# A mixture-of-experts block: the fixed first pass in tiles of 64 and 32 from raw weights, with six loads lent the room of the split parts

## The chip, the cores and the metric

The kernel runs on one core of a Trainium2 chip. It is one launch, and its time is the device time in microseconds (us). The core's engines are TensorE (PE; its weight loads are shown apart as PEld), VectorE (DVE), ScalarE (ACT), GpSimd (POOL) and SyncE (SP), with 16 DMA engines beside them. Each engine runs its own instructions in the order in which the kernel lists them, and waits for other engines by semaphores.

## The reference

The reference is a stack of three blocks over 512 tokens of width 1024: one with convolutions and a linear recurrence, one with attention, and a mixture of experts. The change touches the last alone. In outline:

```
logits = h1 @ w_router + b_router            # 512 tokens, 32 experts
top 4 experts of each token, softmax over the 4 -> gate
for each expert e, on its tokens:
    g, l = split(x @ w_gate_up[e] + b_gate_up[e])     # 1024 -> 2048
    a = swiglu(g, l)                                  # 1024
    out[token] += gate * (a @ w_down[e] + b_down[e])  # 1024 -> 1024
```

All is float32. The weights of one expert are 12 MB, so the 32 experts are 384 MB of the 503 MB that the kernel moves.

## The kernel before

The experts are run in 32 passes. Pass 0 is expert 0 always (`STATIC = 1`); the other experts are put into passes by their number of tokens, so that a pass has a fixed kind. A pass gathers the rows of its tokens from DRAM (an indirect DMA on POOL, `rows_of`, L1571), transposes them on PE, multiplies and scatters the result back. There are four kinds:

- *large* passes hold one tile of 128 places. Their weights are split into a high part (`whi`, cast on ACT, L142) and a remainder (`wlo`, subtracted on DVE, L143), and a unit of 1 MB takes three products of four matmuls each, 128x512 (L1930 for gate_up, L1941 for down). Pass 0 is of this kind.
- *SMALL* passes hold 64 places, from the raw float32 weights (L1912). In the trace a unit has 8 records of a 64-column tile with 512 columns moving.
- *TINY* passes hold 32 places, raw too: 16 records of a 32-column tile with 256 columns moving.
- *PAIRS* (passes 3 and 9) hold 128 places from split weights and 32 more from the raw ones, so each of their units is worked once in either way.

The program goes by blocks. Block b has the 8 gate_up units of pass b and then the 4 down units of pass b-1. Beside them, `beside(b)` lists small work that is put before or in the middle of a given unit: finding the rows of the next pass (`place`, `fetch`), gathering them (`gather`), transposing them (`xpose`, `xparts`), the SwiGLU (`glu`), the transposed activations (`at_T`, `at_parts`) and the scatter (`finish`).

Weights come in loads of 1 MB, all on SP's queue, in the order of use. `Weights` holds a list of loads to do and a list of free buffers (`slots`, 12 in the mixture of experts: 2, 7 from L1351 and 3 from L2062). `issue()` (L117) takes the oldest free slot and puts the next load into it. For a unit that is split, the slot is free again once the two casts have read it, and `split()` issues the next load there; for a raw unit `release(slot)` does that after PE's last product. The high and low parts have buffers of their own, three pairs (`wpart0` to `wpart2`), which serve the layers ahead too. The first 12 loads are gate_up of pass 0 (8) and down of pass 0 (4); then come gate_up of pass 1, gate_up of pass 2, down of pass 1, and so on. From pass 1 on, a load's address depends on `pm_i`, the list of which expert is in which pass; SP reads that into a register with `value_load` and waits for it there.

The stage ahead of pass 0 ends with the normalised rows `hr` being stored to `h_d` (from which the gathers read) and `acc_d` (to which the results are added), also on SP's queue (L1423, L1425). The router's result gives places (`posb`), from which a one-hot (`oh`), PE products with it (`pidx`) and a few DVE operations give the row numbers `ix` of a pass's tokens. Twelve matmuls on a constant (`warm`, L198) stand on PE between that and pass 0.

Of the kernel before, what the change touches and what calls it, by code (L numbers as in the profile page):

```python
# [9 lines left out]
F32 = mybir.dt.float32  # L10
# [4 lines left out]
OP = mybir.AluOpType  # L15
# [19 lines left out]
STATIC = 1  # L35
PAIRS = (3, 9)
SMALL = (1, 2, 4, 6, 8, 10, 12, 14, 16, 18, 20, 22, 24, 26, 27, 28, 29, 30, 31)
TINY = (1, 4, 10)
# [3 lines left out]
def _tables():  # L42
# [35 lines left out]
    for r, q_ in enumerate([*PAIRS, *large, *[q_ for q_ in SMALL if q_ not in TINY], *TINY, *range(STATIC)]):  # L78
        moe[:, q_] = r
        moe[:, 32 + q_] = 160 if q_ in PAIRS else 32 if q_ in TINY else 64 if q_ in SMALL else 128  # L80
    moe[:, 64] = p // 64
# [10 lines left out]
class Weights:  # L92
# [3 lines left out]
    def __init__(self, nc, pools, slots):  # L96
        self.nc, self.slots = nc, list(slots)
        self.parts = [(pools, f"wpart{i}") for i in range(2)]
        self.todo, self.raw, self.part = [], [], []
        self.last, self.used = 0, 0  # L100

# [48 lines left out]
    def release(self, slot):  # L150
        self.slots.append(slot)
        self.issue()

# [17 lines left out]
def block_kernel(ctx, tc, A, out, dbg=None, upto=99):  # L171
# [60 lines left out]
    def kn(k, n):  # L232
        return lambda t: t[:, :k * n].rearrange("p (k n) -> p k n", k=k)
# [58 lines left out]
    for p in range(NE):  # L292
        k = 1 + (p in PAIRS)
        PASSES.append(list(range(ni, ni + k)))
        ni += k
# [10 lines left out]
    def paired(p):  # L306

        return p not in PAIRS and p not in TINY

# [3 lines left out]
    def add_unit(p, dn, u, of, late=0):  # L313
        def src():
            w = of(p)[dn]
            return rows2(w[256 * u:256 * u + 256, :], paired(p)) if dn else w[128 * u:128 * u + 128, :]
        W.add((kn(2, 1024) if dn else flat, src), split="both" if p in PAIRS else p not in SMALL,
              late=late)
# [1145 lines left out]
    for hf in range(2):  # L1464
# [3 lines left out]
        for i in range(4):  # L1468
# [17 lines left out]
            if hf:  # L1486
                stats1(i)
                if i:
                    top4(i - 1)
                else:  # L1490
                    W.ahead(1)
            elif i == 1:
                biases()
            elif i == 2:
                W.ahead(1)
                next(terms)
            elif i == 3:
                next(terms)
    logits_T(3)
    norm1(3)  # L1500
# [82 lines left out]

    oh_ = onehot(posb[:, :, 0:1])
    first = rows_of(rows_at(oh_, lambda i: aux[:, :, i, 0], 0, 2))

# [180 lines left out]
    def small(n):  # L1767

        if PASS_OF[n] in TINY or PLACES[n][1]:
            return 4  # L1770
        return 2 if PASS_OF[n] in SMALL else 0

# [37 lines left out]
    def xpose(n):  # L1810
        it = its[n]
        if small(n):
            it["pt"] = transposed_rows(it["xg"])
        else:
            pt = pss("pxt") if n == 0 else None
            it["pt"] = [transposed(it["xg"], a, pt[:, a, :] if n == 0 else psa("pxt")) for a in range(2)]

# [74 lines left out]
    def small_products(n, dn, u, w, half):  # L1892
# [15 lines left out]
        for k in range(2):  # L1908
# [4 lines left out]
            if k == 0:  # L1913
                half()
        W.release(slot)

# [30 lines left out]
    def beside(b):  # L1947
# [23 lines left out]
        if b == 0:  # L1971
            before[4].append((place, 1))
            midst[4].append((fetch, 1))
            before[5] += [(gather, 1), (late_gates, 0)]
            before[8].append((place, 2))
            midst[7].append((xpose, 1))
            before[8].append((xparts, 1))
        else:
# [29 lines left out]
    def further_tiles():  # L2008
# [4 lines left out]
        with tc.For_i(0, total, 1) as it:  # L2013
            with tc.manual_schedule():
# [48 lines left out]
    W.prefetch()  # L2063
    its[0] = {"oh": oh_, "cols": lambda i: aux[:, :, i, 0], "ix": first[0], "xg": first[1],
              "se": selr[:, 0:1].to_broadcast([128, 128]), "acc": {}, "ac": {}, "pa": {}, "parts": {}}
    for p, dn, u in units(1):
# [7 lines left out]
    warm(12, bias_p)  # L2074
    xpose(0)
    xparts(0)
    for b in range(NE + 1):
# [120 lines left out]
```

## Time and profile before

| | |
|---|---|
| time, median of 3 runs | 1894.53 us (1890.97 to 1894.7) |
| profiled execution, its own time | 1889.37 us |
| its span in the profile | 1887.6 us |
| mean granted clock of PE | 0.951 of full speed |
| PE busy | 1682.0 us, 89% |
| DVE busy | 1127.2 us, 60% |
| ACT busy | 752.8 us, 40% |
| DMA | 503.49 MB, 267 GB/s over the span |

The mixture of experts takes the time from about 800 us on. A busy engine is not a bound by itself: the share is an average over stages with different limits. Which one ends last in a stage is read from what each engine waits for there, and from how full the DMA engines are in it (a share of 1.00 means that all 16 have packets at all times).

### The profile page before, as it was taken

The numbers are of one execution on the slowest core, as the hardware profiler recorded it, in microseconds if no ns is written. First come the engines' busy times: TensorE is split into PE (matmuls) and PEld (weight loads), VectorE is DVE, ScalarE is ACT, GpSimd is POOL, SyncE is SP. The second block draws the span as 40 slices with busy tenths as digits, with TensorE's granted clock in tenths as the row PEclk, the third lists the DMA queues.
The fourth block names the chain that finished last, engine by engine and source line by source line (L and its number), as shares of the span: only waits on it lengthen the run. The fifth ranks groups of instructions, "written<-read, shape, count | busy, mean of one in ns | idle before, by whom it ended". The sixth has DMA issues, their size and how long they took to land. (4 is left out here: it accounts for less than half of the span.)

```text
span 1887.6 us, 22807 instructions
## 1 busy us (share of the span) xinstructions
PE 1682.0 (89%) x8479; PEld 1120.8 (59%) x8479; DVE 1127.2 (60%) x1467; ACT 752.8 (40%) x894; POOL 512.6 (27%) x400
## 2 busy tenths in 40 slices
PE   4899785979998899978999999999999999999885
PEld 3687573758787677854565565666456556642221
DVE  6799983775746555756565466566547545641113
ACT  5233542742335545333354354445335534520001
POOL 3899994550311221311111101110011011110102
PEclk8999897989999899989899999999999999999998
DMA  8322221336131003769999999999999999999993
GB/s 300 90 73 73 78 90 45 111 133 210 59 109 56 1 1 111 296 266 364 379 394 410 399 413 397 394 403 414 418 404 407 406 404 393 405 407 397 407 414 136
DMA packets 127442, 503.49 MB, mean 267 GB/s; under 512 B 15227, under 2 KB 57785, under 8 KB 79713
## 3 DMA queue, kind: packets, MB, share of 16 engines
q1 hardware_dynamic: 115568, 475.24, 63.7%
q0 software_dynamic: 11024, 25.39, 4.9%
q8 instruction: 68, 1.11, 0.2%
q10 hardware_dynamic: 736, 1.38, 0.2%
q14 instruction: 46, 0.37, 0.1%
HBM read 488.56 MB, written 19.84 MB: 269 GB/s over the span
## 5 line engine op out<-in xcount | busy, mean ns | idle before, releaser
L143 DVE TENSOR_TENSOR wlo<-wraw,whi 128x2048 fp32r<-128x2048 f32 (+1 forms) x201 | 456.9, 2282 | 177.8 <-ACT whi L142 172.1
L142 ACT CAST whi<-wraw 128x2048 fp32r<-128x2048 f32 (+1 forms) x201 | 379.5, 1890 | 222.2 <-DMA wraw<-w_down 93.9
L1912 PE MATMUL pg<-wraw,xTs 128*64 128x512 f32 (+1 forms) x1664 | 277.1, 518 | 15.0 <-DMA wraw<-w_gate_up 14.8
L1912 PEld LDWEIGHTS pg<-wraw,xTs 128*64 128x64 f32 (+1 forms) x1664 | 85.5, 126 | 166.2 <-issue 109.8
L1912 PE MATMUL pg<-wraw,ats 128*64 128x512 f32 (+1 forms) x832 | 146.2, 527 | 8.9 <-DMA wraw<-w_down 6.7
L1660 DVE TENSOR_SCALAR lp<-pg 128x512 f32<-128x512 f32 (+1 forms) x47 | 31.1, 661 | 191.9 <-ACT sg L1659 190.3
L563 POOL TENSOR_TENSOR acc<-acc,sparel 128x512 f32<-128x512 f32 x91 | 133.3, 1465 | 7.7 <-ACT acc L552 0.2
L1667 POOL DMA_INDIRECT acc_d<-y,back x20 | 33.1, 1656 | 374.9 <-ACT y L1886 357.1
L1571 POOL DMA_INDIRECT xg<-h_d,ix x34 | 53.9, 1584 | 235.3 <-PE pg L1912 109.8
L1930 PE MATMUL pg<-whi,xTh 128*128 128x512 f32 x416 | 117.1, 403 | 0.4 <-issue 0.4
L1930 PE MATMUL pg<-whi,xTl 128*128 128x512 f32 x416 | 115.8, 400 | 0.0
L1930 PE MATMUL pg<-wlo,xTh 128*128 128x512 f32 x416 | 113.3, 394 | 0.0
L1667 POOL DMA_INDIRECT acc_d<-y,ix x13 | 26.1, 2011 | 309.0 <-ACT y L1889 210.2
L556 DVE SCALAR_TENSOR_TENSOR pc<-v,C,pc 128x512 f32<-128x512 f32 x144 | 101.6, 747 | 2.1 <-ACT pc L552 0.8
L1659 ACT ACTIVATE sg<-pg 128x512 f32<-128x512 f32 (+1 forms) x47 | 25.7, 573 | 183.4 <-PE pg L1912 99.9
L561 POOL TENSOR_SCALAR sparel<-v,C 128x512 f32<-128x512 f32 x91 | 93.8, 1031 | 14.5 <-DVE V L478 5.8
L1930 PEld LDWEIGHTS pg<-whi,xTh 128*128 128x128 f32 x416 | 76.3, 189 | 26.5 <-issue 10.3
L1930 PEld LDWEIGHTS pg<-wlo,xTh 128*128 128x128 f32 x416 | 78.9, 190 | 17.9
L1930 PEld LDWEIGHTS pg<-whi,xTl 128*128 128x128 f32 x416 | 77.3, 190 | 16.6
L1941 PE MATMUL pg<-whi,ath 128*128 128x512 f32 x208 | 73.9, 438 | 12.8 <-ACT whi L142 12.8
L1912 PEld LDWEIGHTS pg<-wraw,ats 128*64 128x64 f32 (+1 forms) x832 | 41.2, 127 | 73.7 <-issue 47.6
L1941 PE MATMUL pg<-wlo,ath 128*128 128x512 f32 x208 | 71.7, 428 | 11.8 <-DVE wlo L143 11.8
(661 smaller groups left out, 3289.3 us busy)
## 6 DMA issues: line engine op xcount, KB each, us to landing
wraw<-w_gate_up SPq DMA_DIRECT2D x256, 1024.0 KB, 20.5
wraw<-w_down SPq DMA_DIRECT2D x128, 1024.0 KB, 21.7
wraw<-w_in SPq DMA_DIRECT2D x17, 1024.0 KB, 5.3
wraw<-w_out SPq DMA_DIRECT2D x8, 1024.0 KB, 6.1
mraw<-mod_w SPq DMA_DIRECT2D x7, 1024.0 KB, 12.5
wraw<-w_in SPq DMA_DIRECT2D x14, 512.0 KB, 5.1
wraw<-pw_w SPq DMA_DIRECT2D x4, 1024.0 KB, 5.2
wraw<-mod_w SPq DMA_DIRECT2D x4, 1024.0 KB, 5.1
```

What stands on the lines that cost most here:

```text
L142: self.nc.scalar.copy(out=hi[:, c], in_=t[:, c])
L143: self.nc.vector.tensor_tensor(out=lo[:, c], in0=t[:, c], in1=hi[:, c].bitcast(F32), op=OP.subtract)
L556: dve.scalar_tensor_tensor(out=acc[:, c, :] if j == 29 and not np_ else st_["o"], in0=v[:, j:j + S], scalar=dw_col(j, c), in1=st_["o"], op ...
L561: pool.tensor_scalar(out=pr_, in0=v[:, j:j + S], scalar1=dw_col(j, c), scalar2=0.0, op0=OP.mult, op1=OP.add)
L563: pool.tensor_tensor(out=acc[:, c, :], in0=acc[:, c, :], in1=pr_, op=OP.add)
L1571: pool.indirect_dma_start(out=xg, out_offset=None, in_=h1_d[:, :], in_offset=bass.IndirectOffsetOnAxis(ap=ix[0:w], axis=0), bounds_check=S ...
L1659: act.activation(out=sg, in_=v2[:, :, :, 0], func=AF.Sigmoid, scale=1.702)
L1660: dve.tensor_scalar(out=lp, in0=v2[:, :, :, 1], scalar1=-6.0, scalar2=8.0, op0=OP.max, op1=OP.min)
L1667: pool.indirect_dma_start(out=dst, out_offset=bass.IndirectOffsetOnAxis(ap=ix, axis=0), in_=y, in_offset=None, bounds_check=nt * S - 1, oo ...
L1912: pe.matmul(o, l, t[:, c0:c0 + n_], start=False, stop=u == 3 and k == 1 if dn else u == 7)
L1930: pe.matmul(it["acc"][c // 2][:, c % 2, :], l, r[:, 512 * c:512 * c + 512], start=False, stop=u == 7 and j == 2)
L1941: pe.matmul(it["acc"][2][:, c, :], l, r[:, c0:c0 + 512], start=False, stop=end)
```

## The change

- The places of expert 0 are 96 and not 128, as a tile of 64 and a tile of 32. Both use the raw weights. `PASSES[0]` has two members, and all that indexed pass 1 by number goes by `PASSES[1][0]`.
- A raw unit of a pass with two tiles is released after the last of them. The down weights of pass 0 are loaded in two pieces of 4 KB for each partition (`128x2x1024`) in place of one of 8 KB.
- Pass 0 has no casts on ACT and no subtractions on DVE: 12 of either go.
- Two one-hots, two sets of row numbers and two gathers stand ahead of pass 0, where one of each stood. The offsets of the second tile's places are a DVE operation more (`pl1`).
- `W.lend()`, called after the last product of the attention block's output layer, puts the six halves of the part buffers on the list of free slots, once: they are not given back by `release`. Three of them take the three down loads of pass 0 that had no room, the other three the first gate_up loads of pass 1. There are 18 slots for the loads up to then, and 12 after.

```
--- before.py
+++ after.py
@@ -77,7 +77,7 @@
     large = [q_ for q_ in range(STATIC, NE) if q_ not in PAIRS and q_ not in SMALL]
     for r, q_ in enumerate([*PAIRS, *large, *[q_ for q_ in SMALL if q_ not in TINY], *TINY, *range(STATIC)]):
         moe[:, q_] = r
-        moe[:, 32 + q_] = 160 if q_ in PAIRS else 32 if q_ in TINY else 64 if q_ in SMALL else 128
+        moe[:, 32 + q_] = 160 if q_ in PAIRS else 32 if q_ in TINY else 64 if q_ in SMALL else 96 if q_ < STATIC else 128
     moe[:, 64] = p // 64
     moe[:, 65] = p // 32
 
@@ -97,7 +97,7 @@
         self.nc, self.slots = nc, list(slots)
         self.parts = [(pools, f"wpart{i}") for i in range(2)]
         self.todo, self.raw, self.part = [], [], []
-        self.last, self.used = 0, 0
+        self.last, self.used, self.lent = 0, 0, []
 
     def add(self, *loads, split=True, n=2048, pieces=1, late=0):
 
@@ -148,8 +148,15 @@
         self.rest = [lambda i=i: piece(i) for i in range(1, pieces)]
 
     def release(self, slot):
-        self.slots.append(slot)
-        self.issue()
+        if slot not in self.lent:
+            self.slots.append(slot)
+            self.issue()
+
+    def lend(self):
+
+        self.lent = [(pool, tag + x) for pool, tag in self.parts for x in "hl"]
+        self.slots += self.lent
+        self.prefetch()
 
     def ahead(self, n):
         while len(self.part) < n and self.ready():
@@ -290,7 +297,7 @@
 
     PASSES, ni = [], 0
     for p in range(NE):
-        k = 1 + (p in PAIRS)
+        k = 1 + (p in PAIRS or p < STATIC)
         PASSES.append(list(range(ni, ni + k)))
         ni += k
     NI = ni
@@ -305,7 +312,7 @@
 
     def paired(p):
 
-        return p not in PAIRS and p not in TINY
+        return p not in PAIRS and p not in TINY and p >= STATIC
 
     def rows2(w, pairs):
         return w.rearrange("(p k) n -> p k n" if pairs else "(k p) n -> p k n", p=128)
@@ -314,7 +321,7 @@
         def src():
             w = of(p)[dn]
             return rows2(w[256 * u:256 * u + 256, :], paired(p)) if dn else w[128 * u:128 * u + 128, :]
-        W.add((kn(2, 1024) if dn else flat, src), split="both" if p in PAIRS else p not in SMALL,
+        W.add((kn(2, 1024) if dn else flat, src), split="both" if p in PAIRS else p not in SMALL and p >= STATIC,
               late=late)
 
     def add_block(b, of):
@@ -1496,6 +1503,7 @@
                 next(terms)
             elif i == 3:
                 next(terms)
+    W.lend()
     logits_T(3)
     norm1(3)
     logits(3)
@@ -1581,8 +1589,14 @@
         dve.scalar_tensor_tensor(out=gt, in0=pi_[:, 2:3], scalar=pi_[:, 3:4], in1=pi_[:, 4:5], op0=OP.add, op1=OP.add)
         return gt
 
-    oh_ = onehot(posb[:, :, 0:1])
-    first = rows_of(rows_at(oh_, lambda i: aux[:, :, i, 0], 0, 2))
+    first = []
+    for nt, p0 in ((2, 0), (4, 64)):
+        pl = posb[:, :, 0:1]
+        if p0:
+            pl = pK.tile([128, 4], F32, name="pl1").unsqueeze(2)
+            dve.tensor_scalar(out=pl, in0=posb[:, :, 0:1], scalar1=float(p0), scalar2=None, op0=OP.subtract)
+        oh_ = onehot(pl, nt)
+        first.append((oh_, *rows_of(rows_at(oh_, lambda i: aux[:, :, i, 0], 0, 2), nt)))
 
     cnt = pK.tile([128, NE], F32, name="cnt")
     pmr = pK.tile([128, NE], F32, name="pmr")
@@ -1768,7 +1782,7 @@
 
         if PASS_OF[n] in TINY or PLACES[n][1]:
             return 4
-        return 2 if PASS_OF[n] in SMALL else 0
+        return 2 if PASS_OF[n] in SMALL or PASS_OF[n] < STATIC else 0
 
     def place(n):
         p, k = PLACES[n]
@@ -1812,8 +1826,7 @@
         if small(n):
             it["pt"] = transposed_rows(it["xg"])
         else:
-            pt = pss("pxt") if n == 0 else None
-            it["pt"] = [transposed(it["xg"], a, pt[:, a, :] if n == 0 else psa("pxt")) for a in range(2)]
+            it["pt"] = [transposed(it["xg"], a, psa("pxt")) for a in range(2)]
 
     def x_tile():
         return [pM.tile([128, 8, 128], F32R, tag=t, name=t) for t in ("xTh", "xTl")]
@@ -1912,7 +1925,8 @@
                 pe.matmul(o, l, t[:, c0:c0 + n_], start=False, stop=u == 3 and k == 1 if dn else u == 7)
             if k == 0:
                 half()
-        W.release(slot)
+        if n == PASSES[PASS_OF[n]][-1]:
+            W.release(slot)
 
     def products(n, dn, u, w, half):
         it = its[n]
@@ -1969,12 +1983,14 @@
                 before[9 if b else 8].append((glu, n, 1))
         nxt = PASSES[b + 1] if b + 1 < NE else []
         if b == 0:
-            before[4].append((place, 1))
-            midst[4].append((fetch, 1))
-            before[5] += [(gather, 1), (late_gates, 0)]
-            before[8].append((place, 2))
-            midst[7].append((xpose, 1))
-            before[8].append((xparts, 1))
+            n1, n2 = PASSES[1][0], PASSES[2][0]
+            before[4].append((place, n1))
+            midst[4].append((fetch, n1))
+            before[5].append((gather, n1))
+            before[3] += [(late_gates, 0), (late_gates, 1)]
+            before[8].append((place, n2))
+            midst[7].append((xpose, n1))
+            before[8].append((xparts, n1))
         else:
             for j, n in enumerate(nxt):
                 if j:
@@ -2061,8 +2077,10 @@
 
     W.slots += [(pM, f"wraw{RAW + RAWK + i}") for i in range(RAWX)]
     W.prefetch()
-    its[0] = {"oh": oh_, "cols": lambda i: aux[:, :, i, 0], "ix": first[0], "xg": first[1],
-              "se": selr[:, 0:1].to_broadcast([128, 128]), "acc": {}, "ac": {}, "pa": {}, "parts": {}}
+    for n, (oh_, ix, xg) in enumerate(first):
+        its[n] = {"oh": oh_, "cols": lambda i: aux[:, :, i, 0], "ix": ix, "xg": xg, "acc": {}, "ac": {}, "pa": {},
+                  "parts": {}}
+        selectors(n)
     for p, dn, u in units(1):
         if not dn:
             add_unit(p, dn, u, of, -4)
@@ -2072,8 +2090,9 @@
     next(ordering)
     W.ahead(3)
     warm(12, bias_p)
-    xpose(0)
-    xparts(0)
+    for n in PASSES[0]:
+        xpose(n)
+        xparts(n)
     for b in range(NE + 1):
         before, midst = beside(b)
         for j, (p, dn, u) in enumerate(units(b)):
```

The rows that follow list SP's instructions in program order, around the stores of the normalised rows (`h_d`, `acc_d`) and the reading of `pm_i`; `wraw` are the weight loads. Before:

```order
L117 DMA wraw<-w_down 128x2048 x2
L1423 DMA h_d<-hr 128x1024 x2
L1425 DMA acc_d<-hr 128x1024 x2
L1423 DMA h_d<-hr 128x1024
L1423 DMA h_d<-hr 128x512 x2
L1425 DMA acc_d<-hr 128x1024 x2
L117 DMA wraw<-w_down 128x2048 x2
L1999 TENSOR_LOAD pm_i
```

And SP after the change, the same place:

```order
L117 DMA wraw<-w_down 128x2x1024
L1430 DMA h_d<-hr 128x1024 x2
L1432 DMA acc_d<-hr 128x1024 x2
L1430 DMA h_d<-hr 128x1024
L117 DMA wraw<-w_down 128x2x1024 x3
L1430 DMA h_d<-hr 128x512 x2
L1432 DMA acc_d<-hr 128x1024 x2
L2015 TENSOR_LOAD pm_i
```

Three loads of 1 MB have moved from both sides of the stores to a place ahead of the last two `h_d` stores, those of the last 128 rows.

On PE, the rows from the `warm` matmuls to the third unit of pass 0 (`pxt` are the transposes of the gathered rows `xg`, `pg` the accumulators, `wraw` the raw weights, `whi` and `wlo` the split ones). Before:

```order
L198 MATMUL warm<-bias_p 128x512 x12
L1650 MATMUL pxt<-sq_107,xg_5233 128x128 x8
L1374 MATMUL pg<-bias_p,selr 128x512 x4
L1930 MATMUL pg<-whi,xTh 128x512 x4
L1930 MATMUL pg<-whi,xTl 128x512 x4
L1930 MATMUL pg<-wlo,xTh 128x512 x4
L1930 MATMUL pg<-whi,xTh 128x512 x4
```

And PE after the change:

```order
L205 MATMUL warm<-bias_p 128x512 x12
L1659 MATMUL pxt<-sq_107,xg_5233 128x64 x8
L1659 MATMUL pxt<-sq_107,xg_5234 128x32 x8
L1919 MATMUL pg<-bias_p,se 128x512 x2
L1925 MATMUL pg<-wraw,xTs 64x512 x4
L1919 MATMUL pg<-bias_p,se 128x256 x4
L1925 MATMUL pg<-wraw,xTs 32x256 x8
L1925 MATMUL pg<-wraw,xTs 64x512 x4
L1925 MATMUL pg<-wraw,xTs 32x256 x8
```

A unit was three products of four; it is now one of a 64-column tile and one of a 32-column tile, in turn. (In the trace each `L1912` matmul of these has two records.)

## Rows read from the trace of the kernel before

**Rows 1.** Stretches: us, busy time by engine, PE clock, DMA share, GB/s.

```profile
820.00:840.00 20.00, 19.59 (x93) 15.62 (x93) 14.45 (x20) 10.83 (x6) 2.81 (x1) 1.00 0.81 313
840.00:860.00 20.00, 15.35 (x166) 9.97 (x166) 9.03 (x18) 6.35 (x9) 0.95 (x1) 0.91 0.49 182
903.00:934.00 31.00, 31.00 (x209) 20.87 (x206) 16.47 (x20) 11.72 (x8) 5.35 (x4) 0.93 1.02 411
934.00:944.00 10.00, 8.49 (x53) 4.28 (x55) 5.21 (x9) 1.84 (x4) 0.00 (x0) 1.00 0.74 255
1145.00:1700.00 555.00, 532.68 (x2616) 326.64 (x2614) 321.91 (x337) 249.12 (x224) 64.48 (x37) 0.97 1.01 405
```

**Rows 2.** Timeline of SP's queue, 800 to 945: start, us, DMAs issued.

```profile
800.67 5.00 SPq L1423 DMA_DIRECT2D h_d<-hr  x3
...
813.37 47.63 SPq L117 DMA_DIRECT2D wraw<-w_gate_up  x16
...
909.90 28.38 SPq L117 DMA_DIRECT2D wraw<-w_gate_up  x8
```

**Rows 3.** What PE waited for, 816 to 944: total us, times, longest.

```profile
PE pxt L1645 <- DMA xg<-h_d,ix: 3.9, 2, 2.7
PE pxt L1645 <- DVE xTl L215: 3.4, 1, 3.4
...
PE pxt L1650 <- DMA xg<-h_d,ix: 0.9, 1, 0.9
```

**Rows 4.** Timeline of PE, starts of blocks: start, us, instruction [idle before].

```profile
815.51 1.03 PE L1650 MATMUL pxt<-sq,xg 128*128 128x128 f32 x8
...
819.84 1.17 PE L1930 MATMUL pg<-whi,xTh 128*128 128x512 f32 x4 [0.38 <-issue]
...
848.18 1.05 PE L1906 MATMUL pg<-bias_p,se 128*128 128x256 f32 x4
...
860.32 0.49 PE L1374 MATMUL pg<-bias_p,selr 64*128 64x512 f32 x2
...
874.26 0.62 PE L1906 MATMUL pg<-bias_p,se 128*128 128x512 f32 x2
```

**Rows 5.** Timeline of PE, units of raw passes and of a PAIR pass.

```profile
855.43 4.96 PE L1912 MATMUL pg<-wraw,xTs 128*32 128x256 f32 x88
...
881.99 7.95 PE L1912 MATMUL pg<-wraw,xTs 128*64 128x512 f32 x36
...
909.77 1.20 PE L1930 MATMUL pg<-whi,xTh 128*128 128x512 f32 x4
910.81 1.09 PE L1930 MATMUL pg<-whi,xTl 128*128 128x512 f32 x4
911.73 1.10 PE L1930 MATMUL pg<-wlo,xTh 128*128 128x512 f32 x4
912.76 1.07 PE L1912 MATMUL pg<-wraw,xTs 128*32 128x256 f32 x16
913.76 1.19 PE L1930 MATMUL pg<-whi,xTh 128*128 128x512 f32 x4
```

**Rows 6.** DMA transfers, at 757.5, 808 and 857: size, us to landing.

```profile
moe<-t_moe SPq DMA_DIRECT2D x1, 52.0 KB, 16.8
...
q0 software_dynamic: 144, 0.13, 12.9%
...
xg<-h_d,ix POOLq DMA_INDIRECT x1, 3.4
...
xg<-h_d,ix POOLq DMA_INDIRECT x1, 8.8
```

**Rows 7.** Timeline of DVE, the first one-hot and the cast of `pm_i`.

```profile
805.04 0.69 DVE L1546 TENSOR_TENSOR oh<-sq,posb 128x512 bf16<-128x512 f32 x1
...
808.77 0.18 DVE L1605 CAST pm_i<-pperm 1x32 int32<-1x32 f32 x1 [1.15 <-PE pperm L1604]
```

**Rows 8.** Timeline of POOL, the gather of pass 0.

```profile
808.42 1.12 POOL L1571 DMA_INDIRECT xg<-h_d,ix  x1 [4.99 <-DVE Pk L1601]
```

More of the change, by code (lines that the diff above doesn't have):

```diff
@@ L79, in _tables @@
         moe[:, q_] = r
-        moe[:, 32 + q_] = 160 if q_ in PAIRS else 32 if q_ in TINY else 64 if q_ in SMALL else 128
+        moe[:, 32 + q_] = 160 if q_ in PAIRS else 32 if q_ in TINY else 64 if q_ in SMALL else 96 if q_ < STATIC else 128
     moe[:, 64] = p // 64
@@ L99, in __init__ @@
         self.todo, self.raw, self.part = [], [], []
-        self.last, self.used = 0, 0
+        self.last, self.used, self.lent = 0, 0, []
     def add(self, *loads, split=True, n=2048, pieces=1, late=0):
@@ L150, in release, with lend @@
     def release(self, slot):
-        self.slots.append(slot)
-        self.issue()
+        if slot not in self.lent:
+            self.slots.append(slot)
+            self.issue()
+    def lend(self):
+        self.lent = [(pool, tag + x) for pool, tag in self.parts for x in "hl"]
+        self.slots += self.lent
+        self.prefetch()
     def ahead(self, n):
@@ L292, in block_kernel @@
     for p in range(NE):
-        k = 1 + (p in PAIRS)
+        k = 1 + (p in PAIRS or p < STATIC)
         PASSES.append(list(range(ni, ni + k)))
@@ L306, in paired @@
     def paired(p):
-        return p not in PAIRS and p not in TINY
+        return p not in PAIRS and p not in TINY and p >= STATIC
     def rows2(w, pairs):
@@ L316, in src @@
             return rows2(w[256 * u:256 * u + 256, :], paired(p)) if dn else w[128 * u:128 * u + 128, :]
-        W.add((kn(2, 1024) if dn else flat, src), split="both" if p in PAIRS else p not in SMALL,
+        W.add((kn(2, 1024) if dn else flat, src), split="both" if p in PAIRS else p not in SMALL and p >= STATIC,
               late=late)
@@ L1498, in block_kernel @@
                 next(terms)
+    W.lend()
     logits_T(3)
@@ L1582, in gates_of @@
         return gt
-    oh_ = onehot(posb[:, :, 0:1])
-    first = rows_of(rows_at(oh_, lambda i: aux[:, :, i, 0], 0, 2))
+    first = []
+    for nt, p0 in ((2, 0), (4, 64)):
+        pl = posb[:, :, 0:1]
+        if p0:
+            pl = pK.tile([128, 4], F32, name="pl1").unsqueeze(2)
+            dve.tensor_scalar(out=pl, in0=posb[:, :, 0:1], scalar1=float(p0), scalar2=None, op0=OP.subtract)
+        oh_ = onehot(pl, nt)
+        first.append((oh_, *rows_of(rows_at(oh_, lambda i: aux[:, :, i, 0], 0, 2), nt)))
     cnt = pK.tile([128, NE], F32, name="cnt")
@@ L1770, in small @@
             return 4
-        return 2 if PASS_OF[n] in SMALL else 0
+        return 2 if PASS_OF[n] in SMALL or PASS_OF[n] < STATIC else 0
     def place(n):
@@ L1814, in xpose @@
         else:
-            pt = pss("pxt") if n == 0 else None
-            it["pt"] = [transposed(it["xg"], a, pt[:, a, :] if n == 0 else psa("pxt")) for a in range(2)]
+            it["pt"] = [transposed(it["xg"], a, psa("pxt")) for a in range(2)]
     def x_tile():
@@ L1914, in small_products @@
                 half()
-        W.release(slot)
+        if n == PASSES[PASS_OF[n]][-1]:
+            W.release(slot)
     def products(n, dn, u, w, half):
@@ L1971, in beside @@
         if b == 0:
[L1972 to L1977, printed above, removed]
+            n1, n2 = PASSES[1][0], PASSES[2][0]
+            before[4].append((place, n1))
+            midst[4].append((fetch, n1))
+            before[5].append((gather, n1))
+            before[3] += [(late_gates, 0), (late_gates, 1)]
+            before[8].append((place, n2))
+            midst[7].append((xpose, n1))
+            before[8].append((xparts, n1))
         else:
@@ L2063, in block_kernel @@
     W.prefetch()
-    its[0] = {"oh": oh_, "cols": lambda i: aux[:, :, i, 0], "ix": first[0], "xg": first[1],
-              "se": selr[:, 0:1].to_broadcast([128, 128]), "acc": {}, "ac": {}, "pa": {}, "parts": {}}
+    for n, (oh_, ix, xg) in enumerate(first):
+        its[n] = {"oh": oh_, "cols": lambda i: aux[:, :, i, 0], "ix": ix, "xg": xg, "acc": {}, "ac": {}, "pa": {},
+                  "parts": {}}
+        selectors(n)
     for p, dn, u in units(1):
@@ L2074, in block_kernel @@
     warm(12, bias_p)
-    xpose(0)
-    xparts(0)
+    for n in PASSES[0]:
+        xpose(n)
+        xparts(n)
     for b in range(NE + 1):
```

## The prediction, made before the changed kernel ran

> **What bounds the kernel now.** I read the stretches of the mixture of experts first [rows 1], then SP's queue [rows 2], then what PE waited for [rows 3], then where its blocks begin [rows 4].
>
> The stretches show three regimes. In 820 to 840 PE is busy 19.59 of 20 us while the DMA share is 0.81, and in 840 to 860 the share is 0.49: the transfers have room, PE sets the pace. From 1145 to 1700 it is the other way: share 1.01 at 405 GB/s, so a load of 1.05 MB every 2.59 us sets the pace. Between them, in 934 to 944, the share falls to 0.74 although every load still ahead is known. SP's queue says why: the eight loads from 909.90 on go out over 28.38 us, one in 28.38 / 7 = 4.05 us, which is PE's pace through pass 3, a PAIR pass, where a unit takes 913.76 - 909.77 = 3.99 us [rows 5]. DMA needs 2.59 for what PE frees in 4.0, so it catches up, all 12 slots are full, and it waits for PE. In 903 to 934 PE is busy for all of the 31.00 us and waits for nothing.
>
> So the state at 944 is "12 slots full, PE in the middle of pass 3", whatever lead the loads had before. What is behind 944 moves by as much as PE's chain from the start of pass 0 to there moves. That shift, d below, is the whole effect on the time; d is made of the start of pass 0 and the lengths of the blocks "gate_up of 0", "gate_up of 1" and "down of 0". They begin at 819.84, 848.18 and 860.32, and the next at 874.26: 28.34, 12.14 and 13.94 us [rows 4].
>
> **The start of pass 0.** Before, the gather went out at 808.42 [rows 8] and took 3.4 us [rows 6]: it landed at 811.8, hidden behind the `warm` matmuls, and the transposes began at 815.51 [rows 4]. Now three loads stand on SP's queue ahead of the last two `h_d` stores, and a gather reads what these store. The three stores of before go out from 800.67 on, the last by 805.67 [rows 2], and the gather follows 2.75 us behind it. The three loads go out right behind the first of these stores, about 801 to 802.5, and take 3 x 2.59 = 7.8 us of the DMA engines: until about 809.5. If the queue is served in order, the 0.5 MB of stores moves until 810.8 and the gathers are issued, with what is left of the 2.75 us, about 812.5 and 1.1 us later (POOL was busy 1.12 us with one), so 813.6. That the order holds is likely: a transfer of 52 KB behind loads on this queue took 16.8 us to land [rows 6]. A gather takes 3.4 us among few transfers and 8.8 among loads [rows 6]; the lent loads are among the few, the next ones come after `pm_i`; I take 6.6, between the two: 820.2. Sixteen transposes take some 0.8 us: the first bias matmul at 821.0, against a first product at 819.84: +1.2.
>
> The bounds. DVE has eight operations more ahead of `pm_i`, a second pass through one-hot, counts and row numbers: before, from the first one-hot at 805.04 to `pm_i` it was 3.7 us for the whole list [rows 7]; I count 2.1 more. `warm` stands behind a product that waits for that list, so it cannot end before 815.5 + 2.1 = 817.6; with the transposes the start is at 818.4 at the earliest: -1.4. With 8.8 us for the second gather it is 823.2: +3.4, and PE's clock may be low after the idle time. The later `pm_i` costs nothing else: the first nine gate_up and down loads are there, and the lent ones need 2.59 us each.
>
> **Gate_up of pass 0.** Twelve units in all (eight here, four in down) change from split to raw. A unit of 64 places takes 7.95 x 8 / 36 = 1.77 us, one of 32 takes 4.96 x 16 / 88 = 0.90 [rows 5], together 2.67. A unit of split weights is three groups of four matmuls; 911.73 - 910.81 = 0.92 for one [rows 5], so 2.76. Equal, but for the switching between the two tile shapes. The PAIR unit shows it: 3.99 less 2.76 less 0.90 leaves 0.33 for two changes. It is between 128 and 32 places; between 64 and 32 none is in the trace. I take half: 2.67 + 0.18 = 2.85, with ends 2.67 and 3.00, which for 12 units is -2.2 and +1.8.
>
> The Trainium skill, page TensorEngine Tiling (Array Packing), section Key Properties, says that changing the tiling mode drains TensorE, which speaks against a pass that changes it twice in each unit. The trace agrees as far as PAIR units go, with the 0.33 us; by the rule a unit would be 3.00 and d would be 1.8 us later than what I forecast, 1895.9 in place of 1894.1.
>
> The block after: 8 x 2.85 = 22.8. The bias of the 64-tile takes 0.6 by the row at 874.26 [rows 4], that of the 32-tile about as much, 1.1 together; before, the bias lay in the time ahead of 819.84. Small products beside it (the permutation, row numbers, transposes of pass 1) 1.4. Then the gather of pass 1. Before, PE waited 2.7 us for it [rows 3], and the clock in 840 to 860 was 0.91, a loss of about 1.8 us around that wait. The gather is issued at the same unit, by a DVE that has no casts to do, so somewhat earlier, into busier DMA engines; I take half of the wait, 1.4, and 0.7 for the clock (ends 0 and 0; 2.7 and 1.8). Sum 22.8 + 1.1 + 1.4 + 1.4 + 0.7 = 27.4, against 28.34: -0.9. The 12 casts and 12 subtractions that go stood beside PE's work here (DVE 14.45 and ACT 10.83 of the 20 us in which PE had 19.59 [rows 1]), so they give nothing themselves.
>
> **Gate_up of pass 1** has the same instructions, and weights that are there either way: 12.14, no change. Three of its loads come from lent slots, in 813 to 825 and not after `release`.
>
> **Down of pass 0.** Bias 0.9, four units 11.4, transposes of pass 2 0.6, row numbers 0.3: 13.2, against 13.94. The difference of -0.7 is mainly the gather wait of 3.9 - 2.7 = 1.2 us [rows 3], which I let go, since DVE has its row numbers sooner; if it stays, +1.2. PE's later wait of 3.4 us for DVE's transposed low part [rows 3] hangs on a DVE list that follows PE's blocks; it moves with them.
>
> **Sum.** d = 1.2 - 0.9 + 0 - 0.7 = -0.4. The profiled execution took 1889.37 us (span 1887.6), so it would be 1889.0. The median of the runs shown, 1894.53, is 5.2 above it; with the same d it becomes 1894.1. The ends by the bounds: start -1.4, units 2.67, no wait for gathers and no clock loss: d = -0.4 - 2.6 - 2.2 - 2.1 = -7.3; start +3.4, units 3.00, all waits and the clock as before: d = -0.4 + 2.2 + 1.8 + 2.4 + 1.2 = +7.2. Hardly all at once; half of it either way is what I expect, 1889 to 1899.
>
> **Rival A: the lead in loads is kept.** If what is behind 944 is bound by DMA from further ahead than I think, then filling idle DMA time is worth itself: 0.19 x 20 = 3.8 us in 820 to 840 and 0.51 x 20 = 10.2 in 840 to 860, 14.0 together, which six lent loads (15.5 us) just fill. Time 1880.5. For it: share 1.01 over 555 us. Against it: the share of 0.74 in 934 to 944 with SP's loads 4.05 us apart, which gives the lead back, and a lent slot that isn't returned.
>
> **Rival B, slower: the late gather.** Three loads ahead of the stores make the first gather late; the next loads, free to go once `pm_i` is there, run beside it. It lands after 8.8 us, PE stands idle for some 5 us between `warm` and the transposes, and its clock is low after that, with the loss of 1.8 us seen around the wait of before. d = -0.4 + 2.2 + 1.8 = +3.6 at 8.8 us, and a landing 1 us later than the latest seen gives +4.6: 1899.1. It decides from a start of pass 0 at about 823.5 on. For it: 16.8 us for 52 KB on that queue. Against it: three loads are only 7.8 us, and there were 3.7 us of slack behind the gather.
>
> **Rival C: the change doesn't hold what it needs.** With more than 96 tokens for expert 0 the extra-tile loop would run, with a whole expert's 12 MB, 31 us at least: 1925. Against it: the first gather's window has 0.13 MB on the gathers' queue [rows 6], some 32 rows of 4 KB.
>
> **How the numbers follow.** A difference of 0.2% is 3.8 us, about what runs of this kernel can tell from none. The forecast, with its spread of about 5 us either way, has 0.70: 0.56 within 0.2%, 0.12 faster, 0.02 slower. Rival A has 0.12, faster. Rival B has 0.16: 0.14 slower, 0.02 within. Rival C has 0.02, slower. So 0.24 faster, 0.58 the same, 0.18 slower. The range leaves out most of A and C and the worst of B: 1885.5 to 1899.5.
>
> **What would show it.** Start: the time of the first bias matmul of pass 0, and the landing of the gathers behind the `h_d` stores. Units: 64-and-32 units of 2.67 to 3.00 us apart. Lead: DMA share near 1.0 in 820 to 860, then a lower share somewhere in 860 to 944, with loads some 4 us apart in pass 3 as before. If the share stays at 1.0 through 944 and the end is more than 5 us earlier, the account of the lead was wrong; if pass 0 starts after 823.5, rival B decides.

## The result, and the profile after

The changed kernel takes 1913.95 us (median of 4 runs, 1911.74 to 1919.99) against 1892.75 for the kernel before beside it: a ratio of 1.012, interval 1.0089 to 1.0151. It is slower by some 21 us, where 1894.1 with a range up to 1899.5 was forecast. The profiled execution took 1915.64 us, 26.3 more than the one of before.

Where the 26.3 us arise is read from the times at which the same work starts in both traces. The first load of the experts' weights is issued 0.7 us later than before, and PE is 0.9 us late ahead of pass 0 (an earlier stage; no part of the change). Pass 3 begins on PE at 919.39 and not 902.22, 17.2 later, so 16.3 us arise in passes 0 to 2. The load issued at 957.93 is 16.2 us later than its counterpart at 941.78, the last load of all 25.1: 8.9 us more arise behind pass 3, spread over some 890 us.

The blocks, in PE's timeline of the changed kernel (start, us, instruction, in brackets the idle time before it and what ended it), answering to [rows 4]:

```profile
823.49 2.10 PE L1659 MATMUL pxt<-sq,xg 64*128 64x64 f32 x16 [4.36 <-DMA xg<-h_d,ix]
825.52 1.22 PE L1919 MATMUL pg<-bias_p,se 128*128 128x512 f32 x2
...
843.27 8.68 PE L1925 MATMUL pg<-wraw,xTs 128*32 128x256 f32 x72
851.88 0.68 PE L1659 MATMUL pxt<-sq,xg 32*128 32x32 f32 x8
...
853.48 0.74 PE L1919 MATMUL pg<-bias_p,se 128*128 128x256 f32 x4
...
857.77 0.66 PE L1689 MATMUL pat<-sq,ac 128*128 128x128 f32 x2 [2.01 <-DVE ac L1676]
...
868.31 0.50 PE L1919 MATMUL pg<-bias_p,se 128*128 128x512 f32 x1
...
881.48 0.73 PE L1919 MATMUL pg<-bias_p,se 128*128 128x512 f32 x2
...
896.85 0.27 PE L1561 MATMUL pidx<-aux,oh 128*128 128x5 bf16 x4 [7.66 <-DVE oh L1550]
897.05 10.05 PE L1925 MATMUL pg<-wraw,xTs 128*64 128x512 f32 x36
907.03 0.50 PE L1919 MATMUL pg<-bias_p,se 128*128 128x256 f32 x2
...
919.39 1.22 PE L1381 MATMUL pg<-bias_p,selr 64*128 64x512 f32 x4
```

| block | before | after | difference | forecast |
|---|---|---|---|---|
| start of pass 0 (less the 0.9 us by which PE was late ahead of it) | 819.84 | 824.6 | +4.8 | +1.2 |
| gate_up of pass 0 | 28.34 | 27.96 | -0.4 | -0.9 |
| gate_up of pass 1 | 12.14 | 14.83 | +2.7 | 0 |
| down of pass 0 | 13.94 | 13.17 | -0.8 | -0.7 |
| gate_up of pass 2 | 15.60 | 25.55 | +9.9 | (not thought of) |

Gate_up of pass 2 is not touched by the change, and it loses most: PE waits 7.66 us for DVE's one-hot, and the 36 records behind it take 10.05 us and not 7.95 [rows 5], at a mean clock of 0.76 in 895 to 908 (of two levels, 1.2 and 2.4 GHz: 0.50 in 897 to 901, right behind the idle time, and 0.96 in 901 to 905). DVE's timeline says what it did meanwhile. First before the change, then after it:

```profile
872.97 0.17 DVE L1555 COPY pi<-pidx 128x5 f32<-128x5 f32 x1 [4.12 <-PE pidx L1553]
873.05 0.18 DVE L1717 TENSOR_TENSOR xy<-cnt,moe 128x32 f32<-128x32 f32 x1
```

```profile
880.58 0.17 DVE L1563 COPY pi<-pidx 128x5 f32<-128x5 f32 x1 [9.52 <-PE pidx L1561]
893.15 0.19 DVE L1731 TENSOR_TENSOR xy<-cnt,moe 128x32 f32<-128x32 f32 x1 [12.41 <-DMA acc_d<-y,back]
...
896.10 0.69 DVE L1550 TENSOR_TENSOR oh<-sq,pl 128x512 bf16<-128x512 f32 x1
```

And POOL's timeline (the gather of pass 0, the two scatters of its results) who held it up:

```profile
816.19 1.04 POOL L1579 DMA_INDIRECT xg<-h_d,ix  x1 [11.89 <-DMA h_d<-hr]
...
881.88 1.63 POOL L1681 DMA_INDIRECT acc_d<-y,back  x1 [19.10 <-issue]
886.46 1.57 POOL L1681 DMA_INDIRECT acc_d<-y,back  x1 [2.95 <-DMA acc_d<-y,back]
```

These rows show a chain of three. `xy` (L1731) is the first operation of the list of further tiles; it needs no result of pass 0. But its tile has the tag `yt`, and so has the result `y` of a pass's second tile, which the scatter reads. Before, pass 0 had no second tile. Now DVE must wait until that tile's scatter has landed, this one may only be issued when the scatter of the first tile has landed (both add into `acc_d`), and the one-hot of pass 3 stands behind `xy` on DVE.

The stores and gathers, on SP's queue, answering to [rows 2]:

```profile
801.52 0.32 SPq L1430 DMA_DIRECT2D h_d<-hr  x1
801.94 1.83 SPq L117 DMA_DIRECT2D wraw<-w_down  x3
805.74 0.81 SPq L1430 DMA_DIRECT2D h_d<-hr  x2
...
925.93 28.51 SPq L117 DMA_DIRECT2D wraw<-w_gate_up  x8
```

The last two stores of `h_d` landed at 814.6 and 815.3, 8.9 and 9.1 us behind their issue; the gathers went out at 816.19 and 817.54 and landed at 823.4 and 824.4. The eight loads issued during pass 3 go out over 28.51 us, as they did over 28.38: PE sets their pace there, as forecast. In the stretches (as [rows 1]) DMA is busier early, falls to a share of 0.46 in 853 to 868, and is slower, not idler, at the end, 400 GB/s at the same share of 1.01 as 405 before:

```profile
804.00:814.00 10.00, 2.75 (x36) 2.36 (x36) 6.87 (x29) 0.00 (x0) 0.30 (x1) 0.50 0.99 356
...
820.00:840.00 20.00, 16.51 (x114) 7.15 (x114) 2.80 (x11) 2.52 (x4) 0.00 (x0) 0.83 0.96 365
840.00:860.00 20.00, 17.40 (x157) 6.48 (x155) 4.97 (x13) 1.77 (x5) 0.90 (x1) 0.92 0.83 315
853.00:868.00 15.00, 12.40 (x154) 5.75 (x146) 5.16 (x14) 2.42 (x7) 0.94 (x1) 0.77 0.46 164
...
895.00:908.00 13.00, 11.15 (x54) 3.77 (x58) 8.32 (x17) 0.85 (x2) 2.04 (x2) 0.76 0.62 222
...
1145.00:1700.00 555.00, 529.66 (x2626) 322.30 (x2622) 315.60 (x333) 241.45 (x221) 61.73 (x35) 0.97 1.01 400
```

### The profile page after: what moved, and what is told of

Its sections match the earlier page's. It is cut to its first block, busy times and chain, and to the rows that moved or that the text cites. A ratio compares the mean times of both kernels' runs of the same rounds, so it can differ in the third digit from the quotient of the medians.

```text
span 1913.9 us, 23102 instructions
## 1 busy us (share of the span) xinstructions
PE 1696.8 (89%) x8640; PEld 1109.6 (58%) x8640; DVE 1102.7 (58%) x1463; ACT 730.2 (38%) x883; POOL 514.3 (27%) x402
## 5 line engine op out<-in xcount | busy, mean ns | idle before, releaser
L143 DVE TENSOR_TENSOR wlo<-wraw,whi 128x2048 fp32r<-128x2048 f32 (+2 forms) x189 | 431.7, 2293 | 176.9 <-ACT whi L142 166.9
L142 ACT CAST whi<-wraw 128x2048 fp32r<-128x2048 f32 (+2 forms) x189 | 356.7, 1888 | 217.3 <-DMA wraw<-w_down 97.6
L1925 PE MATMUL pg<-wraw,xTs 128*64 128x512 f32 (+1 forms) x1856 | 305.2, 520 | 17.8 <-DMA wraw<-w_gate_up 17.2
L1925 PEld LDWEIGHTS pg<-wraw,xTs 128*64 128x64 f32 (+1 forms) x1856 | 93.1, 127 | 185.5 <-issue 122.2
L1925 PE MATMUL pg<-wraw,ats 128*64 128x512 f32 (+1 forms) x928 | 158.8, 520 | 11.5 <-DMA wraw<-w_down 7.3
L1944 PE MATMUL pg<-whi,xTh 128*128 128x512 f32 x384 | 107.6, 402 | 0.0
L1944 PE MATMUL pg<-whi,xTl 128*128 128x512 f32 x384 | 106.5, 399 | 0.0
L1944 PE MATMUL pg<-wlo,xTh 128*128 128x512 f32 x384 | 104.6, 394 | 0.0
L1944 PEld LDWEIGHTS pg<-wlo,xTh 128*128 128x128 f32 x384 | 72.1, 188 | 17.0
L1944 PEld LDWEIGHTS pg<-whi,xTl 128*128 128x128 f32 x384 | 70.8, 189 | 15.4
```

The costliest lines, as they stand in the source:

```text
L142: self.nc.scalar.copy(out=hi[:, c], in_=t[:, c])
L143: self.nc.vector.tensor_tensor(out=lo[:, c], in0=t[:, c], in1=hi[:, c].bitcast(F32), op=OP.subtract)
L1925: pe.matmul(o, l, t[:, c0:c0 + n_], start=False, stop=u == 3 and k == 1 if dn else u == 7)
L1944: pe.matmul(it["acc"][c // 2][:, c % 2, :], l, r[:, 512 * c:512 * c + 512], start=False, stop=u == 7 and j == 2)
```

## Experiments: the waits ahead of pass 3

The first load of the experts' weights is issued between 751.0 and 757.0 us in the kept traces, a difference that arises in earlier stages. So stages of two traces are compared by their lengths below, not by their clock times. The code is cut at "...".

**e1_y_apart.** Tile 1 is the second tile of pass 0; it gets a buffer that is idle until pass 3. The other tiles keep theirs.

```
 def finish(n):
     ...
-    y = pM.tile([128, 256], F32, tag="yt", name="y") if PLACES[n][1] else ...
+    if n == 1:
+        y = pM.tile([128, 8, 128], F32, tag="atl", name="y").rearrange(...)
+    elif PLACES[n][1]:
+        y = pM.tile([128, 256], F32, tag="yt", name="y")
+    else: ...
```

> Only the buffer of the result of pass 0's second tile changes: it no longer shares its buffer with xy, the first tile of the list of further tiles. Theory (shared buffer): DVE no longer waits for the scatter, PE's wait for the one-hot in gate_up of pass 2 (7.7 us) goes, and so does the low clock behind it (the 36 records take 8.0 and not 10.05 us): about 10 us less than the changed kernel, 1904. Rival (late loads: DVE's operation only happens to stand there, and pass 2 is held up by weights that come late): PE then waits for w_gate_up in its place, 1912 to 1914.

1906.58 us (ratio to before 1.0082, 1.0052 to 1.0112), 7.4 less than the changed kernel; the two intervals overlap, so it is the trace that decides. In it `xy` runs at 884.30 straight behind the copy of `pi`, and gate_up of pass 2 takes from 885.11 to 900.82, 15.7 us as before the change. The shared buffer is shown as the cause of that block's 9.9 us. From the issue of the first of the last three `h_d` stores to pass 3 it is 107.6 us in place of 117.9, 10.2 less; the profiled execution gained only 6.1, since it issued that store 2.8 us later. What PE waited for, first in the changed kernel (800 to 1000; us in total, times, longest):

```profile
PE pidx L1561 <- DVE oh L1550: 11.0, 3, 7.7
PE pxt L1659 <- DMA xg<-h_d,ix: 4.4, 1, 4.4
...
PE pat L1689 <- DVE ac L1676: 2.0, 1, 2.0
```

Then in e1, 800 to 960, with the rows of DVE and PE:

```profile
PE pxt L1659 <- DMA xg<-h_d,ix: 5.5, 1, 5.5
PE pidx L1561 <- DVE oh L1550: 3.3, 2, 1.8
...
PE pat L1689 <- DVE ac L1676: 2.0, 1, 2.0
...
884.30 0.18 DVE L1731 TENSOR_TENSOR xy<-cnt,moe 128x32 f32<-128x32 f32 x1
...
892.95 7.95 PE L1930 MATMUL pg<-wraw,xTs 128*64 128x512 f32 x36
900.82 0.51 PE L1924 MATMUL pg<-bias_p,se 128*128 128x256 f32 x2
```

**e2_y_apart_lend_late.** e1, with the call of `W.lend()` moved:

```
-    W.lend()
     logits_T(3)
     ...
     affine1(3)
+    W.lend()
```

> As e1, and the six buffers are lent after the last stores of the normalised rows, so that the three loads stand behind these on SP's queue. Theory (late gather): the stores land about 4 us sooner, the gathers go out about 811 to 812 and not 816.2, the first bias matmul of pass 0 comes at about 820 and not 825.5: 5 us less than e1, 1899. Rival (the start hangs on DVE's longer list and on warm, not on the stores): the start moves by under 1.5 us, 1903.

1895.33 us (ratio 1.0033, 1.0018 to 1.0049), 11 less than e1. SP's queue now has the stores ahead of the loads:

```profile
803.45 0.80 SPq L1430 DMA_DIRECT2D h_d<-hr  x2
804.29 0.94 SPq L1432 DMA_DIRECT2D acc_d<-hr  x2
805.33 3.02 SPq L117 DMA_DIRECT2D wraw<-w_down  x3
```

And POOL and PE:

```profile
807.10 1.04 POOL L1579 DMA_INDIRECT xg<-h_d,ix  x1 [5.09 <-DVE ix L1574]
...
818.17 0.73 PE L1924 MATMUL pg<-bias_p,se 128*128 128x512 f32 x2
...
844.32 0.74 PE L1924 MATMUL pg<-bias_p,se 128*128 128x256 f32 x4
```

The first gather goes out 3.65 us behind the issue of the last two `h_d` stores and not 10.45 behind it as in the changed kernel, and PE doesn't wait for it. That the three loads ahead of the stores held up the gather is shown. The theory's direction holds, its size was too small. Counted from that issue, the first bias matmul comes 6.2 us sooner than in e1, and gate_up of pass 0 takes 26.15 us and not 28.82: its clock is 1.00 in 818 to 842, where e1 had 0.54 in 830 to 836, behind the wait for the gather. The theory left this second part out. In all, e2 gains 8.1 us on e1 from the stores to pass 3; where the rest of the 11 lies is not shown.

**e3_y_apart_no_lend.** e1, without the call:

```
-    W.lend()
```

> As e1, but nothing is lent: 12 slots from the start. Theory (the lead in loads is given back in pass 3): the same as e2 within 1.5 us, 1899, since the gather is early here too and loads are idle in pass 3 either way. Rival (the lead is kept): lending is worth up to 14 us, so this is 10 or more slower than e2, 1909 to 1913.

1898.3 us (ratio 1.0043, 1.0021 to 1.0064; e2's interval overlaps it). Lending is worth some 3 us here, not clear of none; even the far ends of the two intervals lie under 9 us apart, so the 14 us of a lead that is kept are out. In the one profiled execution the loss against e2 is a gather wait of 3.4 us ahead of pass 3, with DMA at share 1.01 in 860 to 903 against 0.95. The first two rows are e2's and e3's stretch, the third is a wait of e3's PE:

```profile
860.00:903.00 43.00, 40.30 (x290) 17.21 (x286) 25.73 (x45) 10.51 (x14) 6.84 (x5) 0.96 0.95 370
860.00:903.00 43.00, 37.65 (x268) 14.59 (x268) 22.91 (x42) 8.10 (x12) 6.44 (x4) 0.88 1.01 397
...
PE pxt L1663 <- DMA xg<-h_d,ix: 3.4, 1, 3.4
```

**e4_lend_late.** The moved call of e2 alone, in the changed kernel.

> The changed kernel with only the lending moved behind the stores; the shared buffer stays. Theory: 5 us less than the changed kernel, 1909, with the 7.7 us wait still there (the two costs add up). Rival (what the start gains is lost in the wait for the scatter, which ends when it ends): 1913.

1910.57 us (ratio 1.0112, 1.0085 to 1.0139), 3.4 less than the changed kernel, with overlapping intervals. In the trace both costs stand apart, as the theory has it: the wait for the one-hot is there with 7.7 us, and the first bias matmul comes 14.7 us behind the issue of the last two `h_d` stores and not 19.8, 5.1 sooner.

## Experiments: the slower loads

All these variants moved their loads at 400 to 402 GB/s, with or without the waits, so the 8 to 9 us behind 950 had to come from something that no wait shows. What they share is `pl1`: a tile of 16 bytes for each partition, rounded to 32, in the pool pK. That pool ends at a fixed place, so the seven weight buffers in it begin at 134880 and not at 134912. `pad` below is an unused tile; no instruction differs by it.

```
f1  before:        pK.tile([128, 4], F32, name="pad")    # behind the buffers: -32 bytes
g2  before:        pK.tile([128, 16], F32, name="pad")   # -64
h1  before:        pK.tile([128, 16], F32, name="pad")   # ahead of them: they stay
h4  before:        pmr = moe[:, 67:67 + NE]; pad of 16   # +64
h5  before:        pmr = moe[:, 67:67 + NE]              # +128
h7  before:        h5, and cnt in lrep, later in moe     # +256
g3  before:        const.tile([128, 16], F32, ...)       # the five other buffers +64
h6  before:        const.tile([128, 4], F32, ...)        # the five other buffers +32
f2, f3, f4         e2, e2 with the transposes later, the changed kernel: each with a pad of 4
g1, g5, h3         pl = pmr[:, 0:4] in place of the tile pl1, no pad in pK
                   (g1: otherwise f3; h3: otherwise the changed kernel; g5: g1 and the pad of g3)
```

> The kernel before with one more tile of 4 numbers for each partition in the pool pK, which nothing writes or reads: no instruction differs, but the seven weight buffers in that pool begin 32 bytes lower, at 134880 and so on (32 beyond a multiple of 64) and not at 134912 (a multiple of 64). Theory (the place of the buffers slows the loads): the loads of 950 to 1830 take about 1% longer, 8 to 9 us, as in every variant with the tile pl1; 1900. Rival (it comes from the other order in which the slots go round, or from pass 0 being raw): no change, 1892.

> The kernel before with an unused tile of 16 numbers in pK: its seven weight buffers begin 64 bytes lower, at 134848. No instruction differs. Theory (multiples of 128 count): slower than before by most of what the shift by 32 cost (9.3 us), about 6: 1897. Rival (multiples of 64 suffice): no change, 1891.

> The kernel before with an unused tile of 16 numbers in the pool const: all that lies in the pools wp and pM2 moves up by 64 bytes, so that the five weight buffers there, at odd multiples of 64 before, begin at multiples of 128, as the seven in pK do; nothing else differs. Theory (multiples of 128 count for each buffer): another 5/7 of the 6 us is gained: 1886 to 1887. Rival (only a shift of pK as such matters, or 64 suffices): 1891.

> The kernel before with the unused tile of 16 numbers put into pK ahead of the weight buffers and not behind them: the pool grows as in the shift by 64, but the seven buffers and all that lies above keep their places (134912). Theory (the buffers' place): no change, 1890. Rival (the size or lower end of the pool as such): 1896 as with the shift by 64.

> The kernel before with pmr as a part of the tile moe (columns of it that nobody reads any more), which frees 128 bytes, and an unused tile of 16 numbers: the seven buffers begin at 134976, 64 bytes higher. Theory A (multiples of 256 count): slower, 1896. Theory B (offsets of 192 and more beyond a multiple of 256 are the slow ones; the five other buffers are at an offset of 64 and fast): no change, 1890.

> As h4 without the unused tile: the seven buffers begin at 135040, an offset of 128 beyond a multiple of 256. Theory A (multiples of 256): slower, 1896. Theory B (slow from an offset of 192 on): no change, 1890. If this or h4 is slow although the five other buffers are fast at offsets of 64 and of 128, the offset isn't what counts.

> The kernel before with an unused tile of 4 numbers in const: the five buffers in wp and pM2 move up by 32 bytes (32 beyond a multiple of 64), the seven in pK stay at 134912. Theory C (only the seven, above 131072 bytes, mind their place): no change, 1890. Rival (each buffer minds an offset of 32, the five had good places by luck): five sevenths of the 9.3 us of the first shift, 1896.

> The kernel before with pmr and cnt as parts of tiles that are there (moe and lrep), which frees 256 bytes: the seven buffers begin at 135168, 256 higher and again a multiple of 256. Theory A (in pK multiples of 256 are fast): no change, 1890, although h4 and h5, 64 and 128 bytes higher with the same pmr, were 1896. Rival (134912 alone is fast, or the shared pmr costs): 1896.

What was measured. The places are those that the programs give the buffers. The last two columns are from the packets of 8 KB in the trace, 1145 to 1700: their mean time, and the part of them that took 307 to 309 ns.

```
kernel               seven buffers at  ratio to before (interval)    GB/s  mean ns  at 309
before               134912            1                             405   317.1    85%
f1 before, -32       134880            1.0046 (1.0033 to 1.0058)     401   320.6    37%
g2 before, -64       134848            1.0034 (1.0023 to 1.0046)     402   319.4    37%
h4 before, +64       134976            1.0039 (1.0020 to 1.0057)     402   319.6    37%
h5 before, +128      135040            1.0034 (1.0017 to 1.0051)     401   319.9    49%
h7 before, +256      135168            1.0000 (0.9988 to 1.0013)     405   316.9    87%
h1 before, pad ahead 134912            0.9996 (0.9982 to 1.0010)     404   317.1    87%
h6 others +32        134912            0.9998 (0.9986 to 1.0011)     405   316.8    88%
g3 others +64        134912            0.9998 (0.9986 to 1.0010)     405   317.1    88%
changed kernel       134880            1.012  (1.0089 to 1.0151)     400   321.4    36%
```

The same in the stretches, first f1 (only addresses lie between it and the kernel before):

```profile
1145.00:1700.00 555.00, 528.32 (x2591) 324.00 (x2588) 321.86 (x334) 247.55 (x222) 61.75 (x35) 0.97 1.01 401
```

Then h7 (addresses, and the two shared tiles):

```profile
1145.00:1700.00 555.00, 532.50 (x2611) 326.49 (x2605) 321.87 (x336) 248.67 (x224) 63.77 (x37) 0.97 1.01 405
```

In f1, g2 and h4 some 37% of the packets keep their 309 ns, where five of the twelve buffers (42%) did not move; in the order of time, seven or eight slow loads alternate with four or five at 309. The median packet of a slow load takes 312 to 313 ns, a fifth of them 317 to 322. The rival for f1, the order of the slots, fell with f1; "multiples of 64 suffice" fell with g2 and f2; "multiples of 128 count for every buffer" fell with g3; "offsets from 192 on" fell with h4 and h5; "134912 alone" fell with h7. What stands is: the seven buffers in pK are fast at the two multiples of 256 that were tried and slow at the four other places, and the five others, which lie lower, are equally fast at 64, 96 and 128 bytes beyond one. The Trainium skill, page DMA: Bandwidth & Descriptors, section How a descriptor splits into AXI transactions, says that when a descriptor doesn't start at a multiple of 256 bytes, its first transaction starts at the multiple below, and the bytes ahead of the start still cost time; it speaks of reads, and what moved here is where the loads write. For the seven the trace agrees (a median of 312 to 313 against 309 ns); for the five it doesn't. Why these don't mind stays open, and so does why h5, at +128, keeps 49%.

> The changed kernel with nothing but the unused tile of 4 numbers added (buffers at multiples of 64). Theory (the costs add up): 8 to 9 us less than the changed kernel, 1905; the waits before 920 stay. Rival: 1914.

1914.03 us: no change, and the expectation missed. It put the buffers at 134848, a multiple of 64, and its loads go at 401 GB/s, as at 134880; of the places tried in pK only the two multiples of 256 are fast.

> The changed kernel with the tile pl1 as a part of pmr, so that the seven buffers are at 134912 again; all else stays (shared buffer, lending ahead of the stores). Theory: the part of the loss behind 950 goes, 7 to 9 us: 1906; the 16 to 17 us ahead of 950 stay. Rival (the waits and the place of the buffers don't add): 1914.

1910.15 us (ratio 1.0095, 1.0062 to 1.0129). In the trace the loads keep pace with those of the kernel before: they are 17.8 us late at the load that goes out at 941.78 before, and 18.7 at the 340th, where the changed kernel went from 16.2 to 24.1; the waits ahead are there as in the changed kernel. The time of the four runs shows only half of that, with a spread of 7.7 us between them and an interval that overlaps the changed kernel's.

## A version that beats both

> e2 (result of the second tile apart, lending behind the stores) with one more unused tile of 4 numbers in pK, so that with pl1 it makes 64 bytes: the weight buffers begin at multiples of 64 again. Theory (place of the buffers): 8 to 9 us less than e2, 1887, with the loads of the DMA-bound part at the pace of the kernel before. Rival (order of slots, raw pass 0): 1895 as e2.

1895.12 us (ratio 1.0014, 0.9998 to 1.0029): missed, for the reason given for f4.

**f3_e2_aligned_at_T** adds, for the transposes of the activations of pass 0's first tile:

```
+            d = int(n == 0)
             for c in range(4):
-                midst[(0, 0, 2, 2)[c]].append((at_T, n, c))
-                before[(1, 1, 3, 3)[c]].append((at_parts, n, c))
+                midst[(0, 0, 2, 2)[c] + d].append((at_T, n, c))
+                before[(1, 1, 3, 3)[c] + d].append((at_parts, n, c))
```

> As f2, and the transposes of the first tile's activations stand one unit later in gate_up of pass 1, since in the changed kernel PE waits 2.0 us there for DVE's SwiGLU of that tile. Theory (a wait on PE ahead of pass 3 counts in full): 2 us less than f2, with gate_up of pass 1 at about 12.9 us and not 14.9; 1885. Rival (covered by something else on the way, or the wait only moves): as f2.

1890.93 us, 4.2 less than f2 (3.2 in the means of the ten runs each). In the trace the wait of 2.0 us became 1.0, and gate_up of pass 1 went from 14.7 us in f2 to 11.65, with the low clock behind the wait gone as well:

```profile
PE pat L1690 <- DVE ac L1677: 1.0, 1, 1.0
```

> As f3, but the tile pl1 is a part of a tile that is there anyway (pmr), and no unused tile stands in pK: its seven weight buffers begin where they do in the kernel before, 134912 (a multiple of 128 and 256); in f3 they begin at 134848 (a multiple of 64 alone), in the changed kernel at 134880 (of 32 alone). Theory (multiples of 128 count): the loads of the DMA-bound part go at the pace of the kernel before, 6 us less than f3: 1885, ahead of the kernel before by what passes 0 to 2 gain. Rival (the order of slots, or raw pass 0, costs the 6 us that alignment to 64 left): 1891 as f3.

1883.95 us (ratio 0.9972, 0.9958 to 0.9987): 405 GB/s, as expected. This is the change with its four costs mended (the shared buffer, the loads ahead of the stores, the early transposes, the place of the buffers).

```profile
1145.00:1700.00 555.00, 532.26 (x2580) 322.95 (x2571) 321.19 (x333) 246.68 (x218) 65.26 (x36) 0.98 1.01 405
```

> As g1, with the unused tile of 16 numbers in const: all 12 weight buffers at multiples of 128. Theory: as much below g1 as the kernel before with all at 128 is below the kernel before, 4 to 5 us: 1881. Rival: as g1.

1882.84 us (ratio 0.9960, 0.9946 to 0.9974), the fastest that was run; against g1 no difference that the intervals show, which fits g3.

## Why the prediction was wrong

- *The sum of blocks.* The step "d is made of the start of pass 0 and the lengths of the blocks" of gate_up 0, gate_up 1 and down 0 failed first and worst: the largest term, 9.9 us, lies in gate_up of pass 2. The prediction followed engines and weight slots through the change, but not the small tiles: a second tile in pass 0 is the first user of `yt` ahead of `xy`. e1 shows it.
- *The start of pass 0.* The mechanism was right, the term mis-sized: +4.8 and not +1.2. The three loads were to be through at 809.5, at the 405 GB/s of a full stretch; in 804 to 814 the transfers moved 356 GB/s, and the second load landed only at 811 (8.6 us behind its issue). So the stores behind them landed at 814.6 and 815.3 (810.8 was forecast) and the first gather went out at 816.19 (812.5). The gathers' own time, 7.2 and 6.9 us, was near the 6.6 that was set. The transposes ran at a low clock: 2.10 us for sixteen, and 1.46 in e2 without the wait, where 0.8 was set without a row. Rival B, "the late gather", named this mechanism, with a d of +4.6; e2 shows it.
- *Gate_up of pass 1*, "no change", took 2.7 more: SwiGLU of two tiles stands ahead of the transposes of the first one. f3 shows it.
- *"What is behind 944 moves by as much"* failed by 8.9 us. PE's waits behind 944 are of the same kinds, but each load takes 1% longer, from 32 bytes in a pool. f1, g1 and h3 show it.
- *Right:* a unit of 64 and 32 places took 8.61 us / 3 = 2.87 (843.27 to 851.88; 2.85 forecast: half of the price of switching in a PAIR unit was a guess that came out); down of pass 0 took 13.17 (13.2), without the gather wait that was let go. The lead of the lent loads was not kept, and rival A did not come: e3 shows some 3 us for lending, not 14.
- *Partly luck:* gate_up of pass 0 took 27.96 (27.4). The forecast held 2.1 us for a wait for pass 1's gather and the low clock around it. PE did not wait there (no idle time at 851.88); instead the clock was low behind the late start, which cost about as much (26.15 in e2 without it).

## What to carry to other kernels

When a change gives a step a second instance, list every buffer that the second one is the first to use, and who used that buffer until then: a wait for a scatter's landing can stand on an engine that has nothing to do with it. Loads that "come early anyway" must not stand on the same queue ahead of small stores that a gather waits for: here the stores landed behind the loads. And when a DMA-bound stretch is slower by a per cent with the same share and the same waits, compare the packets' times and the buffers' addresses before looking for a wait.

## What was not expected of the hardware

A packet of 8 KB into one of the seven buffers of pK mostly took 309 ns where the buffer began at a multiple of 256 (two places), and 312 to 313 in the median at -64, -32 and +64 bytes; at +128 about half of all packets were above 309. It costs 6 to 9 us of 1890. The five lower buffers did not mind shifts of 32 and 64. The granted clock fell to 0.50 behind PE's wait of 7.66 us (897 to 901) and behind one of 2.01 (858 to 863), so that mending a wait gained more than the wait: 9.9 us for the first, and 3.1 in f3 for 1.0 us of the second. It does not fall behind every wait: in g1 PE waited 2.44 us at 887 and the clock was 1.00 throughout 885 to 904.
